# Two score maps of a head, placed in different rows of the TensorE array and issued by turns

## The chip, the core and the metric

The kernel runs on one core of a Trainium2 chip. The metric is the device time of one execution in microseconds (us). Times of the profile count from the start of the span of the profiled execution.

## What is computed

Two layers of an encoder trunk on 512 tokens of width 1024, all in float32. Each layer has a token mixer with four branches (differential attention, a pooling mixer, a short convolution, a gated DeltaNet) and then a channel mixer: a dense SwiGLU in the first layer, a mixture of 8 experts in the second. The change is in differential attention. Each of its 4 heads has two score maps with their own queries and keys, each of width 32, and the output takes one softmax minus a multiple of the other:

```
s1 = jnp.einsum('bqhd,bkhd->bhqk', qa, k1).astype(F32) * scale + bias
s2 = jnp.einsum('bqhd,bkhd->bhqk', qb, k2).astype(F32) * scale + bias
a = jax.nn.softmax(s1, axis=-1) - lam * jax.nn.softmax(s2, axis=-1)
return jnp.einsum('bhqk,bkhd->bqhd', a.astype(v.dtype), v)
```

A block is 128 queries against all 512 keys.

## The kernel before

Activations lie with channels on the 128 partitions and tokens along the free dimension. A float32 product is made of three products of parts: each operand is split into a high part (H) and the rest (L), and H·H, H·L and L·H are added up in one PSUM tile. In projections these are lines 326, 327 and 328 (`mm3`), each on a 128x128 weight and 512 moving columns; in the score maps they are three passes of line 1155.

The queries of map 1 of all heads are one tile of 128 partitions (`aqH0`, `aqL0`), 32 partitions for each head; those of map 2 another (`aqH1`, `aqL1`); keys likewise (`akH`, `akL`). A pass of head h contracts over the partitions 32h to 32h+31, so it takes 32 rows of the array (`tile_position=(32 * h, 0)`) and all 128 of its columns. Both maps of a head use the same 32 rows.

`attention` goes over 4 heads and 4 blocks of queries: 16 blocks in a layer, 32 in both, with 64 maps and 192 passes. In a block, for each map: three passes into a PSUM tile `pt` (a pool of four), then on VectorE (DVE) the bias is added and the row's extreme is found in one operation (line 1160, `asc`), then ScalarE (ACT) takes the exponential and its sum (line 1162). When both maps are there: reciprocals (1165, 1166), a scaling on ACT (1167), the weighted sum on DVE (1168, again `asc`), four transposes on TensorE (1171) and the copy of their result (1173). After four blocks of two heads follow the products with the values (1178), where the two heads of a pair take different 64 columns of the array, and a normalisation (1186, 1196).

So that TensorE has work while DVE and ACT go through this chain, `self.fill()` takes steps from a list of generators (`set_fill` in `mixer`): projections of the other branches, six matmuls of 128x512 a step, with their conversions of weights (292 on ACT and 293 on DVE, `wH` and `wL`) and their later work on DVE, ACT and GpSimd (POOL). A block calls `self.fill(FILL_A)`, with FILL_A = 1, after each map and after the transposes. Once attention is done `end_gens` and later stages take the steps that are left, so their sum is fixed. The code's order is not the order on the engines: the instructions are put in order for each engine when the kernel is built, and on each engine that order is then kept.

The order of the weights' columns in `w_in`, which decides the partition that each query and key lands on, is prepared by `lay` on the host.

Of the kernel before, what the change touches and what calls it, by code (L numbers as in the profile page):

```python
# [17 lines left out]
P = 128  # L18
# [47 lines left out]
FILL_A = 1  # L66
# [67 lines left out]
def col(a):  # L134

    a = np.asarray(a)
    return np.moveaxis(a.reshape(a.shape[:-1] + (-1, P)), -1, 0).reshape(P, -1)


def chunks(w, width):  # L140

    K, M = w.shape
    return np.ascontiguousarray(w.reshape(K // P, P, M // width, width).transpose(2, 1, 0, 3)).reshape(
        M // width, P, -1)
# [8 lines left out]
def lay(inp):  # L153

    f = {k: np.asarray(v) for k, v in inp.items()}
    vec = np.zeros((P, NV), np.float32)

    def put(name, a):
        vec[:, V_OFF[name]:V_OFF[name] + a.shape[1]] = a

    half = np.arange(P) // 64
    put("c", col(f["c"][0]))
    put("ada_b", col(f["ada_b"]))
    put("mix_pre", col(f["norm_mix_pre"]))
    put("mix_post", col(f["norm_mix_post"]))
    put("ffn_pre", col(f["norm_ffn_pre"]))
    put("ffn_post", col(f["norm_ffn_post"]))
    put("b_merge", col(f["b_merge"]))
    put("pool_scale", col(f["pool_scale"]))
    put("sconv_w", np.moveaxis(f["sconv_w"].reshape(NL, 3, 2, P), -1, 0).transpose(0, 1, 3, 2).reshape(P, -1))  # L170
    put("dconv_w", np.moveaxis(f["delta_conv_w"].reshape(NL, 5, 6, P), -1, 0).transpose(0, 1, 3, 2).reshape(P, -1))
    put("subln", np.tile(f["diff_subln"].T, (2, 1)))
    put("dnorm", np.tile(f["delta_norm"].T, (2, 1)))
    for name, key in (("a_log", "delta_a_log"), ("dt_bias", "delta_dt_bias")):
        a = f[key].reshape(NL, 2, 2, 2)
        a = np.repeat(a.transpose(3, 0, 1, 2)[:, :, :, None, :], 2, 3)
        put(name, a[half].reshape(P, -1))
    put("lam", np.broadcast_to(f["diff_lambda"].reshape(1, -1), (P, NL * 128)))
    put("router_b", np.broadcast_to(f["router_b"][0][None], (P, NE)))
    cst, mcst = shape_constants()  # L180
    o = {"vec": vec, "cst": cst, "mcst": mcst,
         "rcst": np.concatenate([np.tile(np.arange(T)[None], (P, 1)), np.arange(P)[:, None] < np.arange(P)[None]],
                                1).astype(np.float32),
         "dist": np.abs(np.arange(P)[:, None] + 384 - np.arange(896)[None]).astype(np.float32)}
    o["x"] = np.ascontiguousarray(f["x"][0].T.reshape(KT, P, T).transpose(1, 0, 2)).reshape(P, KT * T)

    o["ada_w"] = np.ascontiguousarray(f["ada_w"].reshape(NL, D, 6 * KT, P).transpose(0, 2, 3, 1)).reshape(-1, P, D)

    by_hpar = lambda w: w.reshape(2, 2, 64, -1).transpose(1, 0, 2, 3).reshape(256, -1)

    def w_in(l, n, s):
        w = f["w_in"][l][:, s:s + 256]
        return np.ascontiguousarray(by_hpar(w.T).T if n == "dz" else w)
    o["w_in"] = np.concatenate([chunks(w_in(l, n, s), 256) for l in range(NL) for n, s in WIN_ORDER])
    o["w_bg"] = np.stack([chunks(np.ascontiguousarray(f["w_in"][l][:, 2816:2832]), 16)[0] for l in range(NL)])
    o["w_gb"] = np.concatenate([chunks(np.concatenate([f["w_merge"][l, i], by_hpar(f["w_branch"][l, i]) if i == 3
                                                   else f["w_branch"][l, i]]), 256)
                                for l in range(NL) for i in range(4)])
    o["w_o"] = np.concatenate([chunks(f["w_o"][l], 256) for l in range(NL)])
    pw = np.zeros((NL, 2, P, P), np.float32)  # L200
    for l in range(NL):
        for t in range(2):
            for s in range(2):
                pw[l, t, 64 * s:64 * s + 64, 64 * s:64 * s + 64] = f["pool_w"][l, 2 * t + s]
    o["pool_w"] = np.ascontiguousarray(pw.transpose(2, 0, 1, 3)).reshape(P, -1)
    o["ffn_g"] = chunks(f["ffn_w_gate"][0], 256)
    o["ffn_u"] = chunks(f["ffn_w_up"][0], 256)
    d = f["ffn_w_down"][0].reshape(NF // 2, 2, P, 2, 512)
    o["ffn_d"] = np.ascontiguousarray(d.transpose(0, 2, 3, 1, 4)).reshape(NF // 2, P, 2048)
    o["router_w"] = chunks(f["router_w"][0], NE)[0]  # L210
    g = f["moe_w_gate"][0].reshape(NE, 2, 4, P, NF // 2, 256).transpose(0, 4, 1, 3, 2, 5)
    u = f["moe_w_up"][0].reshape(NE, 2, 4, P, NF // 2, 256).transpose(0, 4, 1, 3, 2, 5)
    gu = np.stack([g, u], 5)
    dn = f["moe_w_down"][0].reshape(NE, NF // 2, 1, 2, P, D).transpose(0, 1, 2, 4, 3, 5)
    o["moe_w"] = np.concatenate([gu.reshape(NE, NF // 2, 2, P, 2048), dn.reshape(NE, NF // 2, 1, P, 2048)],
                                2).reshape(NE * 33, P, 2048)
    return o
# [14 lines left out]
class Enc:  # L232
# [899 lines left out]
    def attention(self, l):  # L1132
        nc = self.nc
# [5 lines left out]
        for pr in range(2):  # L1139
            AT = []  # L1140
            for hh in range(2):
                h = 2 * pr + hh
                bias = ap.tile([P, 896], FT, name="abias", bufs=1)
                nc.scalar.activation(bias, dist, AF.Copy, scale=-SLOPES[h])
                at = ap.tile([P, 4, T], FT, name=f"AT{hh}", bufs=1)
                AT.append(at)
                hs = slice(32 * h, 32 * h + 32)
                for qb in range(4):
                    qs = slice(qb * P, qb * P + P)
                    ex, sm = [], self.small.tile([P, 2], FT, name="asum")  # L1150
                    for i in range(2):
                        p = self.pt()
                        q, k = self.qk["q", i], self.qk["k", i]
                        for n, (x, y) in enumerate(((0, 0), (0, 1), (1, 0))):
                            nc.tensor.matmul(p, q[x][hs, qs], k[y][hs, :], start=n == 0, stop=n == 2,
                                             tile_position=(32 * h, 0))
                        self.fill(FILL_A)
                        s = ap.tile([P, T], FT, name="asc", bufs=4)
                        mx = self.small.tile([P, 1], FT, name="amx")
                        nc.vector.tensor_tensor_reduce(s, p, bias[:, 384 - 128 * qb:896 - 128 * qb], -1.0, 3e38,  # L1160
                                                       op0=OP.add, op1=OP.min, accum_out=mx)
                        nc.scalar.activation(s, s, AF.Exp, scale=-1.0, bias=mx, accum_out=sm[:, i:i + 1])
                        ex.append(s)
                    r = self.small.tile([P, 2], FT, name="arc")
                    nc.vector.reciprocal(r, sm)
                    nc.vector.tensor_tensor(r[:, 1:2], r[:, 1:2], self.nlam, op=OP.mult)
                    nc.scalar.activation(ex[1], ex[1], AF.Copy, scale=r[:, 1:2])
                    nc.vector.scalar_tensor_tensor(ex[0], ex[0], r[:, 0:1], ex[1], op0=OP.mult, op1=OP.add)
                    p = self.pt()
                    for kb in range(4):  # L1170
                        nc.tensor.transpose(p[:, kb * P:kb * P + P], ex[0][:, kb * P:kb * P + P], self.ident)
                    self.fill(FILL_A)
                    nc.vector.tensor_copy(at[:, :, qs], p.rearrange("p (b q) -> p b q", b=4))
            p = self.pt()
            for kb in range(4):
                for hh in range(2):
                    h = 2 * pr + hh
                    nc.tensor.matmul(p[64 * hh:64 * hh + 64], self.vt[:, kb, h * 64:h * 64 + 64], AT[hh][:, kb],
                                     start=kb == 0, stop=kb == 3)
# [15 lines left out]
            for b in range(4):  # L1195
                nc.tensor.matmul(pR[:, b * P:b * P + P], rb[:, b].rearrange("p a b -> p (a b)"), self.ident,
                                 start=True, stop=True)
# [1210 lines left out]
```

## Time and profile before

| | |
|---|---|
| Median of three runs | 2623.91 us (2621.54 to 2633.97) |
| Profiled execution: time | 2639.6 us |
| Profiled execution: span | 2637.8 us |
| TensorE (PE) busy | 2503.0 us, 95% of the span |
| DVE, ACT busy | 1605.7 us, 1213.4 us |
| Mean granted TensorE clock | 0.971 of full speed |

The span runs from the first to the last instruction that the profiler recorded; the execution's own time lies 1.8 us above it. TensorE's matmuls are pipelined: one of 512 columns is shown with some 390 ns, though the next starts 230 ns after it. So what a matmul costs the engine is read from start to start, not from the time beside it. A row names the engine, the line of the kernel, the tile written and the tiles read; the passes of a map are the rows of line 1155, and `asc` is written by both 1160 and 1168.

### The profile page before, as it was taken

What the parts mean: (1) busy time and instruction counts of PE and PEld (TensorE: products, weight loads), DVE (VectorE), ACT (ScalarE), POOL (GpSimd) and SP (SyncE); (2) the same over time, 40 slices, a digit from 0 to 9 for tenths busy, and PEclk for the clock granted to TensorE, in tenths of its full rate; (3) what the DMA queues carried; (4) which work ended last, traced back from release to release, by engine and by line L of the source; (5) the groups of instructions that cost most, each with busy time, mean ns of one, the idle gap of its engine ahead of it and who ended that gap; (6) DMA issues with size and microseconds to landing.
All of it is one profiled execution on the core that took longest, in us unless ns stands there. A gap on an engine that the chain in (4) does not pass through costs nothing. (4 is left out here: it accounts for less than half of the span.)

```text
span 2637.8 us, 42408 instructions
## 1 busy us (share of the span) xinstructions
PE 2503.0 (95%) x16106; PEld 2031.3 (77%) x16106; DVE 1605.7 (61%) x2914; ACT 1213.4 (46%) x2153; POOL 306.0 (12%) x304
## 2 busy tenths in 40 slices
PE   7999989989999989999899979999999999999996
PEld 6677767889888788677678878887766767799885
DVE  7666843576555565674734656665565556876685
ACT  4454333433333354544333525554444446765574
POOL 0101321241000021103222110000000001000111
PEclk8999999999999999999899989999999999999998
DMA  7113222454566443121222329557879888975681
GB/s 264 48 65 118 70 71 71 133 192 155 184 200 213 149 149 107 49 66 51 62 79 71 114 92 350 196 206 293 323 294 348 319 315 341 389 270 216 236 319 64
DMA packets 124564, 478.32 MB, mean 181 GB/s; under 512 B 14224, under 2 KB 16912, under 8 KB 97600
## 3 DMA queue, kind: packets, MB, share of 16 engines
q1 hardware_dynamic: 119808, 460.19, 48.8%
q0 software_dynamic: 4544, 15.34, 1.7%
q8 instruction: 128, 2.10, 0.3%
q14 instruction: 84, 0.69, 0.1%
HBM read 462.17 MB, written 13.30 MB: 180 GB/s over the span
## 5 line engine op out<-in xcount | busy, mean ns | idle before, releaser
L326 PE MATMUL mm<-hH,wH 128*128 128x512 f32 (+1 forms) x1264 | 490.4, 390 | 9.0 <-ACT hH L1044 4.8
L328 PE MATMUL mm<-hH,wL 128*128 128x512 f32 (+1 forms) x1264 | 481.7, 381 | 4.4 <-DVE wL L293 4.3
L327 PE MATMUL mm<-hL,wH 128*128 128x512 f32 (+1 forms) x1264 | 481.4, 381 | 1.2 <-DVE hL L1277 1.2
L1842 DVE TENSOR_TENSOR mL<-mraw,mH 128x1024 fp32r<-128x1024 f32 x286 | 343.8, 1222 | 178.3 <-ACT mH L1841 127.0
L292 ACT ACTIVATE wH<-raw 128x512 fp32r<-128x512 f32 (+3 forms) x400 | 246.4, 624 | 433.6 <-PE mm L327 318.1
L293 DVE TENSOR_TENSOR wL<-raw,wH 128x512 fp32r<-128x512 f32 (+3 forms) x400 | 280.0, 716 | 214.1 <-ACT wH L292 210.3
L1841 ACT ACTIVATE mH<-mraw 128x1024 fp32r<-128x1024 f32 x286 | 297.6, 1054 | 153.8 <-PE gu L1865 48.4
L1864 PE MATMUL gu<-hH,mH 128*128 128x384 f32 (+1 forms) x1056 | 313.5, 365 | 2.6 <-DVE hL L1800 1.7
L326 PEld LDWEIGHTS mm<-hH,wH 128*128 128x128 f32 x1264 | 241.7, 191 | 65.7 <-issue 9.9
L328 PEld LDWEIGHTS mm<-hH,wL 128*128 128x128 f32 x1264 | 242.1, 192 | 57.1 <-DVE wL L293 7.2
L327 PEld LDWEIGHTS mm<-hL,wH 128*128 128x128 f32 x1264 | 243.0, 192 | 44.8 <-issue 3.5
L1865 PE MATMUL gu<-hH,mL 128*128 128x192 f32 (+1 forms) x1056 | 268.2, 254 | 0.0
L1864 PEld LDWEIGHTS gu<-hH,mH 128*128 128x128 f32 x1056 | 198.9, 188 | 15.6 <-issue 8.5
L1865 PEld LDWEIGHTS gu<-hH,mL 128*128 128x128 f32 x1056 | 202.2, 192 | 0.8
L1864 PE MATMUL gu<-hL,mH 128*128 128x384 f32 (+1 forms) x704 | 195.6, 355 | 0.0
L1842 DVE TENSOR_TENSOR mL<-f,mH 128x512 fp32r<-128x512 f32 x220 | 140.3, 685 | 73.3 <-ACT mH L1841 57.5
L1865 PE MATMUL gu<-hL,mL 128*128 128x192 f32 (+1 forms) x704 | 172.6, 245 | 0.0
L1841 ACT ACTIVATE mH<-f 128x512 fp32r<-128x512 f32 x220 | 126.4, 621 | 63.0 <-PE gu L1865 39.1
L1864 PEld LDWEIGHTS gu<-hL,mH 128*128 128x128 f32 x704 | 132.6, 188 | 9.1 <-issue 4.9
L1865 PEld LDWEIGHTS gu<-hL,mL 128*128 128x128 f32 x704 | 135.1, 192 | 1.6 <-issue 0.8
L335 DVE CUSTOM_DVE_ANT_0 adr<-adr,ada 128x1024 f32<-128x1024 f32 x56 | 68.6, 1224 | 106.4 <-DMA adr<-in_ada_w 106.4
L326 PE MATMUL mm<-mH,ma 128*128 128x512 f32 (+1 forms) x308 | 126.4, 410 | 0.4 <-ACT ma L1882 0.4
(643 smaller groups left out, 4456.5 us busy)
## 6 DMA issues: line engine op xcount, KB each, us to landing
mraw<-in_moe_w SPq DMA_DIRECT2D x209, 1024.0 KB, 9.6
f<-in_moe_w SPq DMA_DIRECT2D x220, 256.0 KB, 6.8
raw<-in_w_gb SPq DMA_DIRECT2D x64, 640.0 KB, 3.9
adr<-in_ada_w SPq DMA_DIRECT2D x56, 512.0 KB, 3.4
raw<-in_w_in SPq DMA_DIRECT2D x40, 512.0 KB, 3.7
raw<-in_ada_w SPq DMA_DIRECT2D x32, 512.0 KB, 4.3
raw<-in_ffn_d SPq DMA_DIRECT2D x58, 256.0 KB, 3.5
raw<-in_ffn_g SPq DMA_DIRECT2D x24, 512.0 KB, 4.6
```

The source lines that it names most:

```text
L292: self.nc.scalar.activation(h, part, AF.Copy)
L293: self.nc.vector.tensor_tensor(l, part, h, op=OP.subtract)
L326: t.matmul(out, W[0], X[0], start=start, stop=False)
L327: t.matmul(out, W[0], X[1], start=False, stop=False)
L328: self.last_mm = t.matmul(out, W[1], X[0], start=False, stop=stop).ins
L335: self.nc.vector.tensor_tensor_reduce(r, r, self.sc, 1.0, 0.0, op0=OP.mult, op1=OP.add, accum_out=t[:, m:m + 1])
L1841: self.mark(self.nc.scalar.activation(h[:, s], x, AF.Copy))
L1842: self.mark(self.nc.vector.tensor_tensor(l[:, s], x, h[:, s], op=OP.subtract))
L1864: t.matmul(pp[i][:, f, :2 * n], w[0], X[k][:, :, :n], start=k == 0, stop=False)
L1865: self.mark(t.matmul(pp[i][:, f, :n], w[1], X[k][:, 0, :n], start=False, stop=k == KT - 1))
```

## The change

Two edits. On the host the columns of the queries and keys of the second map are rolled by 32 within their 128, so that head h of the second map lies on the partitions of 32((h+1) mod 4), while the first map keeps 32h. In `attention` both PSUM tiles are taken first, the six passes of the two maps are issued by turns (pass 1 of map 1, pass 1 of map 2, pass 2 of map 1, ...), and the two single filling steps behind the maps become one call for two steps behind both. What follows for each map is as it was.

```
     def w_in(l, n, s):
         w = f["w_in"][l][:, s:s + 256]
+        if n in "qk":
+
+            w = np.concatenate([w[:, :P], np.roll(w[:, P:], 32, 1)], 1)
...
-                hs = slice(32 * h, 32 * h + 32)
+                row = [32 * h, 32 * ((h + 1) % 4)]
                 for qb in range(4):
                     qs = slice(qb * P, qb * P + P)
                     ex, sm = [], self.small.tile([P, 2], FT, name="asum")
-                    for i in range(2):
-                        p = self.pt()
-                        q, k = self.qk["q", i], self.qk["k", i]
-                        for n, (x, y) in enumerate(((0, 0), (0, 1), (1, 0))):
-                            nc.tensor.matmul(p, q[x][hs, qs], k[y][hs, :], start=n == 0, stop=n == 2,
-                                             tile_position=(32 * h, 0))
-                        self.fill(FILL_A)
+                    pp = [self.pt() for _ in range(2)]
+                    for n, (x, y) in enumerate(((0, 0), (0, 1), (1, 0))):
+                        for i in range(2):
+                            q, k = self.qk["q", i], self.qk["k", i]
+                            hs = slice(row[i], row[i] + 32)
+                            nc.tensor.matmul(pp[i], q[x][hs, qs], k[y][hs, :], start=n == 0, stop=n == 2,
+                                             tile_position=(row[i], 0))
+                    self.fill(2 * FILL_A)
+                    for i, p in enumerate(pp):
                         s = ap.tile([P, T], FT, name="asc", bufs=4)
```

The added lines move the numbers below them: 1155, 1160, 1168 and 1171 are 1159, 1165, 1173 and 1176 in the changed kernel, and 293, 326 to 328 and 935 are 296, 329 to 331 and 938.

On TensorE, at the second block of the first layer, the order before has two products of a filling projection between the maps (`akH_150` is of the first map, `akH_152` of the second):

```order
L1171 MATMUL pt<-cst,asc 128x128 x4
L1155 MATMUL pt<-akH_150,aqH_146 128x512
L1155 MATMUL pt<-akL_151,aqH_146 128x512
L1155 MATMUL pt<-akH_150,aqL_147 128x512
L327 MATMUL mm<-hL_84,wH 128x512
L328 MATMUL mm<-hH_83,wL 128x512
L1155 MATMUL pt<-akH_152,aqH_148 128x512
L1155 MATMUL pt<-akL_153,aqH_148 128x512
L1155 MATMUL pt<-akH_152,aqL_149 128x512
L326 MATMUL mm<-hH_85,wH 128x512
```

In the changed kernel the same place on TensorE reads:

```order
L1176 MATMUL pt<-cst,asc 128x128 x4
L1159 MATMUL pt<-akH_150,aqH_146 128x512
L1159 MATMUL pt<-akH_152,aqH_148 128x512
L1159 MATMUL pt<-akL_151,aqH_146 128x512
L1159 MATMUL pt<-akL_153,aqH_148 128x512
L1159 MATMUL pt<-akH_150,aqL_147 128x512
L1159 MATMUL pt<-akH_152,aqL_149 128x512
L329 MATMUL mm<-hH_83,wH 128x512
```

The two products have moved behind the maps. Counted over the whole order, 4 of the 16 blocks of each layer (the first four) have filling work between their two maps before, and the other 12 have their six passes side by side already; in the changed kernel all 16 have. The filling products between the last pass of a block and its transposes change too: in the first layer 16, 17, 20, 19, 16, 33, 21, 18, 28, 24, 18, 18, 26, 22, 23, 23 before, and 21, 20, 19, 24, 21, 26, 30, 20, 26, 27, 22, 20, 26, 22, 23, 23 now (the fourth with 38 small matmuls of another branch among them); in the second layer 18, 16, 25, 22, 23, 16, 19, 26 in the last eight before and 22, 18, 20, 25, 21, 20, 21, 26 now.

On DVE, in the third block of the first layer, the end of the block's chain stood behind two conversions before (`x_741` is of the pooling branch):

```order
L1166 TENSOR_TENSOR arc<-arc,nlam 128x1
L931 TENSOR_SCALAR x_741<-dy 64x512
L935 TENSOR_TENSOR x_741<-x_741,cst 128x8 x2
L293 TENSOR_TENSOR wL<-raw,wH 128x512
L1168 SCALAR_TENSOR_TENSOR asc<-asc,arc 128x512
```

In the changed kernel DVE has there:

```order
L1171 TENSOR_TENSOR arc<-arc,nlam 128x1
L934 TENSOR_SCALAR x_741<-dy 64x512
L1173 SCALAR_TENSOR_TENSOR asc<-asc,arc 128x512
L934 TENSOR_SCALAR x_741<-dy 64x512
L296 TENSOR_TENSOR wL<-raw,wH 128x512
L938 TENSOR_TENSOR x_741<-x_741,cst 128x8 x2
```

The weighted sum, for which the transposes wait, has come ahead of the weight conversion and of the two small products. The order is the same there in the second layer.

## Rows read from the trace of the kernel before

**Rows 1.** The page: the span, and TensorE's busy time, share and instructions.

```profile
span 2637.8 us, 42408 instructions
PE 2503.0 (95%) x16106; PEld 2031.3 (77%) x16106; DVE 1605.7 (61%) x2914; ACT 1213.4 (46%) x2153; POOL 306.0 (12%) x304
```

**Rows 2.** Both attention stretches: length; PE, PEld, DVE, ACT, POOL busy; clock; DMA.

```profile
65.16:211.60 146.44, 142.12 (x663) 101.91 (x662) 97.72 (x236) 73.50 (x147) 12.73 (x9) 0.97 0.18 60
1035.05:1182.50 147.45, 143.20 (x653) 102.33 (x652) 97.89 (x236) 73.98 (x147) 12.33 (x9) 0.94 0.17 55
```

**Rows 3.** Waits of TensorE, first attention stretch: us in total, times, longest.

```profile
PE pt L1171 <- DVE asc L1168: 2.9, 1, 2.9
```

**Rows 4.** Timeline of TensorE, second block, layer 1: start, duration, instruction.

```profile
73.74 0.50 PE L327 MATMUL mm<-hL,wH 128*128 128x512 f32 x1
74.08 0.40 PE L328 MATMUL mm<-hH,wL 128*128 128x512 f32 x1
74.40 0.49 PE L1155 MATMUL pt<-akH,aqH 32*128 32x512 f32 x1
74.74 0.39 PE L1155 MATMUL pt<-akL,aqH 32*128 32x512 f32 x1
74.97 0.39 PE L1155 MATMUL pt<-akH,aqL 32*128 32x512 f32 x1
75.29 0.50 PE L326 MATMUL mm<-hH,wH 128*128 128x512 f32 x1
```

**Rows 5.** Timeline of all engines, fifth block of layer 1, from first pass to transposes.

```profile
111.97 0.50 PE L1155 MATMUL pt<-akH,aqH 32*128 32x512 f32 x1
...
112.31 0.40 PE L1155 MATMUL pt<-akL,aqH 32*128 32x512 f32 x1
...
112.98 0.69 DVE L1160 CUSTOM_DVE_ANT_0 asc<-pt,abias 128x512 f32<-128x512 f32 x1 [0.21 <-PE pt L1155]
...
113.26 0.38 PE L1155 MATMUL pt<-akH,aqL 32*128 32x512 f32 x1
113.57 0.51 PE L327 MATMUL mm<-hL,wH 128*128 128x512 f32 x1
...
116.48 0.75 DVE L1168 SCALAR_TENSOR_TENSOR asc<-asc,arc 128x512 f32<-128x512 f32 x1 [0.85 <-ACT asc L1167]
...
117.36 0.38 PE L1171 MATMUL pt<-cst,asc 128*128 128x128 f32 x2
```

**Rows 6.** Line 1178: its durations (ns, min/median/max), then two groups of its timeline.

```profile
L1178 PE MATMUL pt<-AT,avt x64: 592/592/643, 141.0 to 1187.3; 128*64 128x512 f32 x64
...
1112.19 1.07 PE L1178 MATMUL pt<-AT,avt 128*64 128x512 f32 x2
...
1114.09 3.65 PE L1178 MATMUL pt<-AT,avt 128*64 128x512 f32 x14
```

**Rows 7.** Timeline of the third block of layer 1, the end of its chain.

```profile
86.34 0.72 ACT L1167 ACTIVATE asc<-asc,arc 128x512 f32<-128x512 f32 x1 [0.99 <-DVE arc L1166]
...
87.65 0.68 DVE L293 TENSOR_TENSOR wL<-raw,wH 128x512 fp32r<-128x512 f32 x1
...
88.25 1.55 DVE L1168 SCALAR_TENSOR_TENSOR asc<-asc,arc 128x512 f32<-128x512 f32 x1
...
89.85 0.66 PE L1171 MATMUL pt<-cst,asc 128*128 128x128 f32 x4 [2.90 <-DVE asc L1168]
```

**Rows 8.** Two stretches behind that block; columns as in Rows 2.

```profile
90.40:93.70 3.30, 3.30 (x9) 1.06 (x8) 0.63 (x4) 0.00 (x0) 3.04 (x3) 0.50 0.20 78
97.30:104.00 6.70, 6.70 (x28) 5.33 (x26) 2.50 (x11) 4.00 (x8) 0.00 (x0) 0.50 0.00 0
```

**Rows 9.** Timeline of the thirteenth block: DVE behind a projection, and the transposes.

```profile
185.06 0.69 DVE L966 TENSOR_TENSOR dpad<-cc,mm 128x512 f32<-128x512 f32 x1 [1.35 <-PE mm L328]
...
187.87 0.75 DVE L1168 SCALAR_TENSOR_TENSOR asc<-asc,arc 128x512 f32<-128x512 f32 x1
...
188.72 0.61 PE L1171 MATMUL pt<-cst,asc 128*128 128x128 f32 x4
```

## The prediction, made before the changed kernel ran

> **What bounds the kernel now.** Start with the page: TensorE is busy for 95% of the span [rows 1]. That share alone does not price a change to TensorE, so the next view is that of the stretches. The change acts only in two of them, the attention of each layer, 146.4 and 147.5 us long; TensorE is shown busy for 142.1 and 143.2 us there, DVE for 97.7 and 97.9 [rows 2]. Then the list of waits: in the first stretch TensorE waits 2.9 us for DVE's weighted sum, and once only [rows 3]. So TensorE sets the pace, and the filling work, whose sum is fixed, closes nearly every gap: what a block saves on TensorE lets everything behind it start earlier, unless the transposes then have to wait. How near they are to that, the timeline says. In the fifth block the weighted sum ends at 117.23 us and the transposes start at 117.36; in the thirteenth 188.62 and 188.72 [rows 5, 9]. The slack is a tenth of a microsecond: the chain through DVE and ACT is a second bound, just behind the first.
>
> **What a pass and a change of rows cost.** Read from start to start. A pass takes 0.23 us (74.74 to 74.97) [rows 4]. From a 128-row product to a pass it is 0.32, to the next pass 0.34; from the last pass to a product 0.32, and to the next product 0.34 [rows 4]. So each change between 32 and 128 rows costs 0.09 ahead of it and 0.11 behind it, 0.20 in all. In a block whose maps stand side by side the four steps from 112.31 to 113.26 take 0.95, or 0.24 each, with no step between the maps [rows 5].
>
> **The change, part by part.**
>
> *Fewer changes of rows.* In 8 of the 32 blocks filling work stood between the maps, which costs four changes; now there are two. 8 x 0.40 = 3.2 us, whatever else happens.
>
> *Two passes at once.* This term decides, and no row shows two products that take different rows and the same columns. Bounds: the lower is the passes as they are, one behind the other at 0.24, gain nothing. The upper is the nearest row with different tiles by turns, line 1178. Two of its instructions alone take 1.07 us, of 0.59 to 0.64 each, so the second starts 0.43 or more behind the first. Fourteen, the halves of the columns by turns, take 3.65 us; one behind another they would take 13 x 0.43 + 0.59 = 6.2 [rows 6]. So two tiles of the array do work at once. By that, six passes become three steps, and a block saves 3 x 0.24 = 0.71 us; if the second map's first weights lie open like the first's (0.11 [rows 4]), 0.60. I take 0.65, near the upper bound, since line 1178 is the only row where two tiles alternate, and nothing there is lost: 32 x 0.65 = 20.8 us. With the changes of rows, TensorE sheds 24.0 us (at most 25.9, at least 3.2).
>
> The Trainium skill ("TensorE: Matmul & The Clock Gate", part 3 on packing small matmuls) states for row tiles that products start about 4 ns apart and gives 3.07 times the throughput for four products of 32 rows and 512 columns; by that page a pair would cost one pass, 0.71 us less a block. The trace of before agrees for halves of columns and does not show it for rows.
>
> *The stall of the third block.* The weighted sum started at 88.25 us though ACT had finished its input at 87.06; a weight conversion from 87.65 and two small products stood ahead on DVE [rows 7]. Now they stand behind it. It can start up to 1.19 us earlier, in both layers, since the order is the same: 2.4 us (bounds: none, and twice the whole 2.9). What moves behind it, the weight conversion, is due next for a filling projection that comes only behind the next maps.
>
> *The clock.* Behind that stall the granted clock is 0.50 for 3.3 us and again for 6.7 us [rows 8], that is 1.2 of 2.4 GHz, and half of each stretch is lost, 5.0 us. TensorE had stood 2.9 us ahead of the first, and ahead of the second it ran small matmuls, which stay. I take no change; the bounds are 5 us either way.
>
> *What is given back.* The transposes come up to 0.65 us sooner than now and have 0.1 us of slack. Does the chain move too? In the fifth block it hangs on the first map: DVE started 1.01 us after the first pass, when the map's third pass was through [rows 5]. With overlap that pass is again the third step, so the chain stays where it is; but the order now has 21 products there in place of 16, 5 x 0.23 = 1.15 us of cover, and no wait appears. In the thirteenth block there are 26 products as before; but DVE itself sat 1.35 us waiting for a projection there [rows 9], and that projection comes earlier with TensorE, so the chain moves along. A block with neither help waits 0.65 - 0.10 = 0.55. Leaving out the third and fourth blocks, bounds over 28 blocks are 0 and 15.4 us. I take 0.25 each, a little under half, since both kinds of help are seen: 7.0 us.
>
> *At nothing:* the host's rolling of columns (same bytes, same transfers), and the two `pt` tiles taken at once (adjacent maps had two already, from a pool of four). The joined filling steps cost nothing while the sum of steps is fixed; if they left a gap, it would be in the give-back above.
>
> **The sum.** 24.0 + 2.4 - 7.0 = 19.4 us. Against the profiled execution, 2639.6 - 19.4 = 2620.2. That execution was 15.7 us above the median of the runs; off the median, 2623.9 - 19.4 = 2604.5, so **2605 us**, or 0.7% faster.
>
> **The rivals.**
>
> *The chain takes it back.* The passes overlap, but every block then waits for DVE: 24.0 - 15.4 = 8.6 us, 2615. For it: a slack of 0.1 us in both blocks read. Against: DVE is busy for only 67% of the stretches [rows 2], and most orders of the first layer's early blocks got longer cover. The Trainium skill ("TensorEngine Tiling (Array Packing)", section on the PSUM bottleneck) warns of just this: tiling speeds TensorE, not what empties PSUM. The rows above agree that the chain is next.
>
> *No overlap.* Both maps send results to all 128 columns; if that makes the second wait, only the switches and the stall's part remain, 3.2 + 2.4 = 5.6 us. Worse, by turns the first map is ready two steps later, 0.47 us, so the chains start later; the longer cover hides most of it. I leave 4 us: 2620. For it: no row shows shared columns. Against: the columns of line 1178 each have their own rows busy, all 128, so overlap as such is no rarity here.
>
> *Going from one row place to another costs like a change of rows.* Then each block has five more changes of 0.20 us: 32 x 5 x 0.20 = 32 us, less 5.6, so 2650, slower. It decides from 5.6 / 160 = 0.035 us a change. Against it: line 1178 changes its columns with every instruction and loses nothing [rows 6]. For it: a change of rows has its price today [rows 4].
>
> **Chances.** Forecast 0.60; chain takes it back 0.18; no overlap 0.15; slower 0.07. The forecast's own range: 25.9 + 2.4, 5 us of a clock that stays up and nothing given back make 2590.6; a give-back of 11 us makes 2608.5. The range for 8 in 10 reaches over the two weaker gains and leaves out the slower case and the extreme of the gains: **2594 to 2621**. About 0.5%, 13 us, is what a measurement of this kernel can tell from no change; only the forecast lies beyond it: faster 0.60, same 0.33 (the two weak cases), slower 0.07.
>
> **What would show it.** Overlap: in the timeline, the six passes of a block start in three pairs, some 0.24 us between pairs, and from first pass to first product it takes 0.9 us, not 1.6; without it the starts stay 0.24 apart, and with a price on changing places they lie 0.3 or more apart. The give-back: in TensorE's waits, line 1176 for `asc`, 7 us over both stretches if right, 15 if the rival is. The stall of the third block shrinks from 2.9 to under 2 us. Both attention stretches get some 10 us shorter; if they do and the time does not follow, a later stage took it. The forecast is wrong, above all, if a new wait of some 3 us in one block brings the clock down for several microseconds, or if the pairs do not start together.

## The result, and the profile after

The changed kernel takes 2619.09 us (median of 18 runs, 2614.5 to 2625.01), the kernel before 2633.16 (18 runs, 2621.54 to 2638.33). The ratio is 0.9947, 95% interval 0.9938 to 0.9957: 14.1 us or 0.53% faster. The forecast was 19.4 us off a median of three runs that lay 9.2 us under that of the eighteen. The profiled execution took 2621.0 us.

The page of the changed kernel, which answers to [rows 1], has the span and TensorE's busy time:

```profile
span 2619.2 us, 42410 instructions
PE 2478.2 (95%) x16106; PEld 2012.9 (77%) x16106; DVE 1599.8 (61%) x2914; ACT 1211.8 (46%) x2153; POOL 304.1 (12%) x304
```

TensorE issues as many instructions as before and is busy 24.8 us less. The timeline of TensorE in the second block of the first layer, the place of [rows 4], shows where; x2 means two instructions in one row:

```profile
69.59 0.49 PE L1159 MATMUL pt<-akH,aqH 32*128 32x512 f32 x2
69.93 0.39 PE L1159 MATMUL pt<-akL,aqH 32*128 32x512 f32 x2
70.16 0.40 PE L1159 MATMUL pt<-akH,aqL 32*128 32x512 f32 x2
70.49 0.50 PE L329 MATMUL mm<-hH,wH 128*128 128x512 f32 x1
70.82 0.39 PE L330 MATMUL mm<-hL,wH 128*128 128x512 f32 x1
```

The six passes start in three pairs, and from the first to the next product it takes 0.90 us; 1.60 before with maps side by side [rows 5]. In the trace the two starts of the first pair lie 4 ns apart.

The stretches of attention (length; PE, PEld, DVE, ACT, POOL busy; clock; DMA), which answer to [rows 2]:

```profile
62.50:200.80 138.30, 133.22 (x664) 95.13 (x662) 96.50 (x236) 72.81 (x147) 12.36 (x9) 0.95 0.19 63
1028.30:1163.10 134.80, 128.62 (x654) 91.54 (x652) 96.57 (x236) 72.78 (x147) 12.75 (x9) 0.96 0.19 60
```

They are 8.1 and 12.7 us shorter. TensorE's waits there (us in total, times, longest), the first layer's ahead of the second's, stand against the one of [rows 3]:

```profile
PE pt L587 <- DVE g L578: 2.4, 1, 2.4
PE pt L1201 <- DVE bt L1199: 1.4, 1, 1.4
PE pt L1176 <- DVE asc L1173: 1.0, 3, 0.6
...
PE pt L587 <- DVE g L578: 4.0, 1, 4.0
...
PE pt L1176 <- DVE asc L1173: 0.5, 1, 0.5
```

The stall of the third block is gone, and the transposes (line 1176) hardly wait. The first row of each layer is new: line 587 is the cumulated sums of the gates, small products of a filling branch, and it waits for `g` on DVE. (The row of line 1201 stands in both traces of the kernel before too, as line 1196 with 1.3 us.)

Where that wait comes from, the timeline of all engines shows, in the fourth block of the first layer, from its last pass on (in brackets the idle time before, and what ended it):

```profile
85.99 0.40 PE L1159 MATMUL pt<-akH,aqL 32*128 32x512 f32 x2
...
86.94 1.46 DVE L934 TENSOR_SCALAR x<-dy 64x512 f32<-64x512 f32 x1 [0.47 <-POOL dy L928]
88.09 1.47 POOL L928 TENSOR_TENSOR dy<-dy 128x513 f32<-128x513 f32 x1
...
89.59 0.42 DVE L934 TENSOR_SCALAR x<-dy 64x512 f32<-64x512 f32 x1 [1.17 <-POOL dy L928]
90.05 0.24 DVE L938 TENSOR_TENSOR x<-x,cst 128x8 f32<-128x8 f32 x2
90.38 1.28 POOL L939 TENSOR_TENSOR x<-x,dpad 128x512 f32<-128x512 f32 x1 [0.82 <-DVE x L938]
...
91.71 0.68 DVE L1165 CUSTOM_DVE_ANT_0 asc<-pt,abias 128x512 f32<-128x512 f32 x1 [1.41 <-issue]
91.72 0.06 DVE L608 MEMSET dpad<- 128x2 f32 x1
...
97.03 0.19 DVE L578 SCALAR_TENSOR_TENSOR g<-uu,nA 128x32 f32<-128x32 f32 x1
...
97.36 0.40 PE L587 MATMUL pt<-g,cst 64*64 64x16 f32 x6 [2.41 <-DVE g L578]
```

The maps are through at 86.4 us, but the bias step (line 1165) starts at 91.71. In the order built for DVE there stand ahead of it a step of the pooling branch (line 934), which waits for POOL's line 928, and then the clears of the padding of `dpad` (lines 608 and 609), which wait for POOL's line 939; so DVE idles while the finished maps lie there. Everything of the gates behind it is late too; `g` comes at 97.2, 10.9 us after the gates' first small products (86.32), and TensorE has run out of filling work 2.4 us earlier. Before, TensorE came to this block later, at 94.30 us. There `g` came 5.6 us after those products (95.62), and line 584, which is 587 of the changed kernel, found it ready:

```profile
100.98 0.19 DVE L575 SCALAR_TENSOR_TENSOR g<-uu,nA 128x32 f32<-128x32 f32 x1
...
105.50 0.43 PE L584 MATMUL pt<-g,cst 64*64 64x16 f32 x6
```

Three of the four windows of the stretches in which the granted clock is low (columns as in the stretches above), which answer to [rows 8]:

```profile
89.40:92.60 3.20, 3.20 (x9) 2.55 (x8) 1.56 (x8) 0.17 (x1) 1.44 (x2) 0.50 0.00 0
99.30:105.90 6.60, 6.60 (x19) 4.79 (x19) 3.03 (x9) 3.37 (x10) 0.00 (x0) 0.51 0.23 79
...
1062.00:1072.40 10.40, 9.85 (x37) 7.33 (x38) 5.08 (x16) 4.73 (x11) 0.00 (x0) 0.51 0.16 52
```

They are at 0.50 or 0.51, that is 1.2 of 2.4 GHz. The second lies 2 us behind the wait for `g`, and the third begins at the end of that wait in the second layer (line 587 starts at 1062.55). Ahead of the first TensorE ran 64 products of 4 columns from 86.32 to 88.28. The fourth, 3.4 us from 143.8 on, lies behind neither.

### The profile page after: what moved, and what is told of

It is laid out like the page before. It is cut to its first block, busy times and chain, and to the rows that moved or that the text cites. A ratio compares the mean times of both kernels' runs of the same rounds, so it can differ in the third digit from the quotient of the medians.

```text
span 2619.2 us, 42410 instructions
## 1 busy us (share of the span) xinstructions
PE 2478.2 (95%) x16106; PEld 2012.9 (77%) x16106; DVE 1599.8 (61%) x2914; ACT 1211.8 (46%) x2153; POOL 304.1 (12%) x304
```

## The experiments

Ratios are to the kernel before on the same chip, with 95% intervals. The two theories at the start: the gain is two passes running at once, and the issue by turns is what makes it (mine); or it comes from the new order of the filling work and of DVE (the rival). 

### Which part gives the time

**Other order, same rows.** The changed kernel without the rolling, so that both maps of a head have the same 32 rows. On every engine the order is that of the changed kernel.

```
-        if n in "qk":
-            w = np.concatenate([w[:, :P], np.roll(w[:, P:], 32, 1)], 1)
...
-                row = [32 * h, 32 * ((h + 1) % 4)]
+                row = [32 * h, 32 * h]
```

> The changed kernel with one thing taken back: both maps of a head lie in the same 32 rows again; the passes still go by turns, and every engine keeps the order of instructions of the changed kernel. Theory (two passes at once brings the gain): the six passes of a block take 1.6 us to the first product again in place of 0.9, so 32 x 0.69 = 22 us come back on TensorE, less some waits that vanish; 14 to 22 us slower than the changed kernel, ratio to the kernel before 0.999 to 1.004. Rival (the gain comes from the order: fewer changes of rows, the weighted sum ahead of the conversions): ratio stays at 0.995 to 0.997.

Measured: 2640.69 us, ratio 1.0009 (0.9995 to 1.0022). The timeline of TensorE in its second block:

```profile
76.64 0.72 PE L1159 MATMUL pt<-akH,aqH 32*128 32x512 f32 x2
77.21 0.62 PE L1159 MATMUL pt<-akL,aqH 32*128 32x512 f32 x2
77.68 0.62 PE L1159 MATMUL pt<-akH,aqL 32*128 32x512 f32 x2
```

Each pair now takes two steps, and the gain is gone: the order gives nothing by itself. The new wait is there: line 587 waits 0.2 and 1.8 us in the two layers, against 2.4 and 4.0. Part of that difference is the clock. From the gates' first small products to the last product ahead of line 587 TensorE has the same work, without a gap, in both layers of the changed kernel and, below, of this one (columns as in the stretches):

```profile
86.32:94.95 8.63, 8.63 (x87) 6.97 (x85) 4.92 (x22) 2.52 (x7) 4.52 (x4) 0.80 0.16 55
1051.48:1058.51 7.03, 7.03 (x87) 5.81 (x85) 3.62 (x13) 0.88 (x4) 4.55 (x4) 1.00 0.18 63
...
88.16:98.31 10.15, 10.15 (x86) 8.25 (x85) 5.38 (x24) 4.71 (x11) 3.81 (x3) 0.66 0.07 25
1066.58:1075.20 8.62, 8.62 (x86) 6.97 (x85) 4.88 (x21) 3.16 (x8) 3.84 (x3) 0.80 0.07 26
```

(x87 and x86 differ by the end of one pass that reaches into the window.) At full clock (1.00) it takes 7.03 us. What a lower clock adds comes off the wait, since `g` comes no later for it: 10.9 us after the first of those products in both layers of the changed kernel, 10.2 in both here. With that added back, line 587 would wait, by estimate, 4.0 us in both layers of the changed kernel and 3.3 in both layers here. So the wait belongs to the new order, and overlap makes it some 0.7 us a block longer, what it saves on the passes of one block.

**The same rows, one map behind the other.** As above, with the loops over `n` and `i` exchanged:

```
-                    for n, (x, y) in enumerate(((0, 0), (0, 1), (1, 0))):
-                        for i in range(2):
+                    for i in range(2):
+                        for n, (x, y) in enumerate(((0, 0), (0, 1), (1, 0))):
```

> Both maps in the same 32 rows, all three passes of the first map and then those of the second, the two filling steps behind both: the kernel before with only the filling moved. Theory (two passes at once brings the gain): only the changes of rows are saved, 8 x 0.40 = 3.2 us, and some of the stall: ratio to the kernel before 0.997 to 1.000. Rival (order brings it): 0.995 to 0.996.

Measured: 2634.52 us, 0.9993 (0.9979 to 1.0006). Issuing by turns on the same rows neither costs nor gives anything that shows. Line 587 waits 2.9 and 1.3 us.

**Both kernels again**, for a second trace of each.

> The changed kernel once more, for a second profile and on this chip. Theory (the 14 us of the medians are the attention stretches alone, and the 21 us that the two profiles show there are partly the luck of two executions): ratio 0.994 to 0.996, attention stretches within 4 us of 137.7 and 134.2. Rival (a later stage takes some 7 us back each time): stretches as before, and the part between the two attention stretches some 4 us longer than in the kernel before again.

> The kernel before once more, for a second profile. Ratio 0.999 to 1.001. If the first profile was a slow execution, its attention stretches of 145.9 and 147.0 us come out 2 to 5 us shorter here; if the attention gain of 21 us is steady, they stay, and what lies between them is shorter in the kernel before than in the changed one.

Measured: 2622.71 us, 0.9944 (0.9931 to 0.9957) for the changed one; 2635.05, 0.9995 (0.9983 to 1.0007) for the one before. Line 587 waits 4.1 and 2.4 us in the changed one, with the clock at 1.00 and 0.80 on the way there: the two layers have changed places. The stretches of the kernel before are these:

```profile
63.10:209.30 146.20, 141.95 (x664) 101.97 (x662) 98.17 (x236) 73.53 (x147) 12.74 (x9) 0.96 0.18 60
1039.40:1182.15 142.75, 138.49 (x654) 98.68 (x652) 97.81 (x236) 73.86 (x147) 12.33 (x9) 0.98 0.18 57
```

The second is 4.7 us shorter than in [rows 2], at a clock of 0.98 in place of 0.94. The stretches of the changed kernel add up to 273.1 us in both of its traces, so they are 20.8 us shorter than in the first trace of before and 15.9 shorter than in the second. Whether a later stage takes something back is not told by this: between the stretches lie 823 and 830 us before, 828 and 832 in the changed kernel.

**Other rows, one map behind the other.** The changed kernel with only the loops exchanged, as above.

> The second map in other rows as in the changed kernel, but all three passes of the first map come ahead of the three of the second: only the turns are taken back. Theory (the engine starts products in order, and one starts beside the one before it if that is in other rows): in a block only the second map's first pass can start beside the first map's third, one step of 0.24 us of six is saved in place of three, 32 x 0.24 = 7.7 us; ratio to the kernel before 0.996 to 0.998. Rival (the engine runs ahead by itself, turns are not needed): 0.994 to 0.995.

Measured: 2626.84 us, 0.9947 (0.9927 to 0.9967). The whole gain stays, against my theory, and the timeline of TensorE says why:

```profile
110.40 0.50 PE L1159 MATMUL pt<-akH,aqH 32*128 32x512 f32 x2
110.74 0.40 PE L1159 MATMUL pt<-akL,aqH 32*128 32x512 f32 x2
110.97 0.40 PE L1159 MATMUL pt<-akH,aqL 32*128 32x512 f32 x2
111.30 0.50 PE L331 MATMUL mm<-hH,wL 128*128 128x512 f32 x1
```

These are passes 1, 2 and 3, each of both maps, though in the order built for TensorE all three of the first map stand ahead of the second's. The second map's first pass starts at 110.411, 10 ns behind the first map's first and 0.33 us ahead of the first map's second (110.741). The Trainium skill ("TensorE: Matmul & The Clock Gate", Part 3, The mechanism) says that products start strictly in the program's order; this trace differs, and it decides. (The order built for DVE and ACT shifts a little with the loops: line 587 waits 3.5 and 3.6 us, the transposes 2.5 and 3.7.)

**The rows alone.** The kernel before with the rolling and the second map's row place; the order of every engine stays that of before.

```
-                hs = slice(32 * h, 32 * h + 32)
+                row = [32 * h, 32 * ((h + 1) % 4)]
...
-                                             tile_position=(32 * h, 0))
+                                             tile_position=(row[i], 0))
```

> The kernel before with the rows alone: the second map of a head lies in other rows, and nothing is moved; every engine keeps the order of the kernel before. Theory (TensorE starts a product ahead of its turn when its rows are free, so neither turns nor the joined filling are needed for the overlap): in the 24 blocks whose maps stand side by side the six passes start in three pairs, 24 x 0.70 = 17 us less on TensorE; but that order holds fewer products between maps and transposes, and the waits of TensorE for the weighted sum grow by 4 to 10 us: ratio to the kernel before 0.995 to 0.998. Rival (it needs the joined filling and the order that comes with it): 0.998 to 1.0.

Measured: 2626.74 us, 0.9950 (0.9934 to 0.9967), not told apart from the change itself. In the 24 blocks whose maps stood side by side the passes overlap. Steps added up, TensorE sheds 16.4 us, but the waits of the transposes grow. In the first layer (line 1174 is 1176 of the changed kernel):

```profile
PE pt L1174 <- DVE asc L1171: 4.3, 5, 2.9
```

The stall of the third block (2.9) stays, and 1.4 us come to it; so does the second layer with 4.3 us over 4. Its line of the cumulated sums doesn't wait in either layer. The new order of the changed kernel therefore does two things that nearly cancel: it joins the maps of eight blocks and removes that stall, and it brings the wait for `g`.

### Where the rest went

**Cumulated sums later.** If the wait for `g` is lost time, line 587 must come later. The branch is cut at that line, and its second half is due behind the keys' branch.

```
-FILL_ORD = "pbkzqsv"
+FILL_ORD = "pbkBzqsv"
...
+        self.dl = dict(beta=beta, g=g)
+        self.bg_sm = sm
+        yield
+
+    def g_bg2(self):
```

> The changed kernel with one other thing moved: the 12 small products of the gates' cumulated sum (line 587), for which TensorE waits 2.4 and 4.0 us in the changed kernel, are a filling step of their own, two projections later. Theory (a new wait for the gates took back 6.4 us and the clock behind it some 3): 5 to 10 us faster than the changed kernel, ratio to the kernel before 0.9905 to 0.9925. Rival (the waits only move to the transposes of the same block, whose sum hangs on the same DVE queue): 0.994 to 0.995, and the wait of line 1176 grows by what line 587 lost.

Measured: 2623.9 us, 0.9926 (0.9902 to 0.9951), which overlaps the interval of the changed kernel: not settled by the time. The waits, first layer (line 1183 is 1176):

```profile
PE pt L1183 <- DVE asc L1180: 2.8, 2, 2.2
```

Most of the 2.4 us has moved to the next thing that needs the late bias step, the transposes; so it is in the second layer, with 3.0 us.

**And the clears on GpSimd.** Besides, the branches' clears of `dpad` go from DVE to GpSimd.

```
-            nc.vector.memset(pad[:, 0:2], 0.0)
+            nc.gpsimd.memset(pad[:, 0:2], 0.0)
```

> As the one with the cumulated sum later, and the four clears of padding columns go from DVE to GpSimd, so that DVE's queue no longer stands behind the pooling branch's work on GpSimd in the fourth block, where the bias step came 5.7 us after the maps in the changed kernel. Theory (the fourth block's chain is held up by the clears, in order on DVE): the bias step there comes within 2 us of the maps, and another 2 to 6 us go; ratio to the kernel before 0.988 to 0.992. Rival (GpSimd, now with the clears as well, holds up what comes next): no better than 0.9925.

Measured: 2618.39 us, 0.9918 (0.9900 to 0.9936). The bias step comes earlier, but not within 2 us of the maps; DVE's timeline (line 941 is 934 of the changed kernel, 1172 is 1165):

```profile
86.58 1.47 DVE L941 TENSOR_SCALAR x<-dy 64x512 f32<-64x512 f32 x1 [0.47 <-POOL dy L935]
89.23 0.42 DVE L941 TENSOR_SCALAR x<-dy 64x512 f32<-64x512 f32 x1 [1.19 <-POOL dpad L616]
...
89.85 0.69 DVE L1172 CUSTOM_DVE_ANT_0 asc<-pt,abias 128x512 f32<-128x512 f32 x1
```

The last pass ends at 86.0; the bias step starts 3.8 us later (5.3 in the changed kernel), still behind the pooling branch's wait for POOL. With line 587 moved, the largest wait of the transposes is 0.8 us in the first layer and 2.4 in the second, where no half clock lies ahead of it (3.4 us do in the first). The ratio's interval ends at 0.9936, just below the 0.9938 where the changed kernel's first one begins; its second, from 0.9931, overlaps. A gain of 0.3% over the changed kernel is likely, not shown.

**Four maps at once.** If row places run side by side, four should. Both heads of a pair go together: second maps rolled by 64, the four tiles taken at once, twelve passes by turns; the second head's bias is written over `dist`.

```
-            w = np.concatenate([w[:, :P], np.roll(w[:, P:], 32, 1)], 1)
+            w = np.concatenate([w[:, :P], np.roll(w[:, P:], 64, 1)], 1)
...
-                row = [32 * h, 32 * ((h + 1) % 4)]
+                row.append([32 * h, 32 * ((h + 2) % 4)])
...
+                pp = [[self.pt() for _ in range(2)] for _ in range(2)]
```

> Twice the dose: the four maps of two heads lie in the four row places and their twelve passes go by turns, then four filling steps, then the two chains one behind the other. Theory (row places work at once, four like two): twelve passes take three steps, 0.9 us to the first product in place of 2 x 0.9, so 16 x 0.9 = 14 us more go from TensorE; the chain of two blocks is longer than the filling and gives 0 to 10 back: ratio to the kernel before 0.987 to 0.995. Rival (results of four row places to the same columns do not fit, or weights for four do not load in a step): twelve passes take six steps and the ratio is 0.994 to 1.0.

Measured: 2610.74 us, 0.9891 (0.9875 to 0.9907). TensorE's timeline:

```profile
105.95 0.54 PE L1160 MATMUL pt<-akH,aqH 32*128 32x512 f32 x4
106.29 0.43 PE L1160 MATMUL pt<-akL,aqH 32*128 32x512 f32 x4
106.52 0.43 PE L1160 MATMUL pt<-akH,aqL 32*128 32x512 f32 x4
106.89 0.50 PE L329 MATMUL mm<-hH,wH 128*128 128x512 f32 x1
```

Twelve passes take three steps, 0.94 us in all with the change of rows. A new wait again takes its part, the first row of TensorE's waits in the first layer:

```profile
PE pt L557 <- ACT dth L546: 2.9, 1, 2.9
```

Line 557 is the gates' first small products, which wait for ACT; 2.8 us in the second layer.

**Four maps, with the late sums and the clears on GpSimd.**

> Four maps at once as before, with the gates' cumulated sum as a filling step of its own two projections later and the clears of padding on GpSimd. Theory (what is left of the four maps' waits hangs on the gates' chain and on DVE standing behind the pooling branch): 2 to 8 us faster than four maps alone, ratio to the kernel before 0.986 to 0.988. Rival (the wait of 2.9 us for the gates' first small matmuls, which stay where they were, is the one that counts): 0.988 to 0.990.

Measured: 2612.05 us, 0.9900 (0.9882 to 0.9918), no different from four maps alone. The wait of line 557 stands unmoved at 2.9 us; what was mended was not what waited here.

**Four maps, the gates' first products a step of their own as well.** With the edits of the last kernel, and two places later in the filling order, so that ACT has time for `dth`:

```
-FILL_ORD = "pbkzqsv"
+FILL_ORD = "pbkcqBzsv"
...
+    def g_bg1(self, l):
```

> As four maps with the cumulated sum later, and the gates' first small matmuls, for which TensorE waited 2.9 and 2.8 us with four maps, also become a filling step of their own, one projection later. Theory (that wait and the clock behind it cost 5 to 9 us in both layers): ratio to the kernel before 0.984 to 0.987, and no wait of TensorE over 1.5 us in either attention stretch. Rival (the chain through DVE and ACT is the bound by now): 0.987 to 0.989, with the waits of the transposes grown instead.

Measured: 2605.47 us, 0.9885 (0.9865 to 0.9905; four runs), within the noise of four maps alone, and the lowest median of all. It lies where the rival had put it (0.987 to 0.989), though the interval reaches into the theory's range. The wait of line 557 is gone, and those of the transposes have grown from 1.9 and 1.2 us in the two layers to 2.7 and 2.5; the first layer's:

```profile
PE pt L1190 <- DVE asc L1187: 2.7, 3, 1.4
```

## Why the prediction came out as it did

Steps from start to start on TensorE, added up over both stretches, before (second trace) against after (first):

| Term | forecast, us | seen, us |
|---|---|---|
| passes and the changes of rows around them | -24.0 | 55.7 to 31.6: -24.1 |
| gaps ahead of the transposes, third block's stall among them | -2.4 + 7.0 | 13.9 to 12.1: -1.8 |
| wait of line 587 for `g` | 0 | 2.4 + 4.0: +6.4 |
| clock (half of the time at 0.50) | 0 | 17.1 to 23.9: +3.4 |
| steps around the transposes | 0 | +1.2 |
| sum | -19.4 | -14.9 |

The medians say -14.1, and the stretches of these two traces -15.9. Against the first trace of before the stretches give -20.8 and the span -18.6, near the forecast. That is luck: the other terms agree within 0.3 us in both traces of before, but the first was at half clock for 27.3 us in the stretches.

*Two passes at once, and fewer changes of rows:* right, within 0.1 us of 24.0. Line 1178, with its columns by turns [rows 6], was a fair guide to rows by turns. The busy time of the passes alone, in windows around the two stretches, says the same. Before:

```profile
60.00:215.00 155.00, 27.52 (x96) 0.97 0.18 61
1020.00:1190.00 170.00, 28.00 (x96) 0.95 0.18 58
```

And after, 22.8 us less for the same 192 passes:

```profile
60.00:215.00 155.00, 16.57 (x96) 0.96 0.21 68
1020.00:1190.00 170.00, 16.15 (x96) 0.97 0.17 54
```

*The stall of the third block:* right in kind and too small. The weighted sum came ahead of the conversion, and all of the 2.9 us a layer went, not 1.2.

*What is given back:* this is the step that failed in kind. I put 7.0 us on the transposes of 28 blocks and left out the third and fourth. The transposes give back some 4 us (5.8 of stall gone, gaps only 1.8 shorter), with waits of 1.0 and 0.5 us in the list. The loss is in the fourth block, which I had left out: 6.4 us of a filling branch's product that waits for DVE, which itself stands behind POOL. The joined filling steps were put at nothing "while the sum of steps is fixed", but it is not only how many: line 587 now stands where its input isn't ready. That the order brings most of it is shown by the same rows by turns, which wait there without overlap, and by the rows alone, which overlap in the old order and don't wait there. The number hides this error: with the stall I forecast 7.0 - 2.4 = 4.6 us given back, and 6.4 - 1.8 = 4.6 were seen. That is luck.

*The clock:* "no change" is the step that failed in the sum; most of the 5.3 us by which the forecast gain was too large lies here, as far as is known. Single traces can't tell: at half clock in the stretches were 27.3 and 17.1 us in the two traces of before and 23.9 in each of the changed kernel, so the row of the table is +3.4 us against the second trace and -1.7 against the first. The mean granted clock of whole executions tells more. For the kernel before it is 0.9752 (29 runs) and between 0.9747 and 0.9760 in three smaller sets, for the changed one 0.9734 (18 runs) and 0.9732 (5 runs); the standard errors of the 29 and the 18 are 0.0004. A clock lower by 0.0018 over 2620 us is 9.4 us more at half clock, by estimate 4.7 us of time; with that in place of 3.4 the sum is -13.6, and it lies just inside the prediction's bounds of 5 us. Where in the execution it falls the runs don't say. The lower clock goes with the new order and not with overlap: the rows alone stay at 0.9753 (6 runs, 0.9755 before), and the same rows by turns, with order and wait but without overlap, have 0.9722 (12 runs). That the wait for `g` is what brings it down is argued from where the low stretches lie, not shown: four maps at once wait 2.9 us for `dth` and have 0.9752 (6 runs). The prediction named a new wait of some 3 us with the clock behind it as what would make it wrong, but did not price it into the sum.

*The base:* the forecast of 2605 is 14.6 us under the time; 5.3 of that is the gain, and 9.2 the median of three runs. So the larger part of the miss is not the change at all.

*The rivals:* none took place. "The chain takes it back" priced 15.4 us on the transposes, which wait 1.5. "No overlap" falls with the pairs. A price for changing places would have shown in the steps from pair to pair; they are 0.34 and 0.23 us, as with one place [rows 4]. Its sign would have been seen also in the rows alone, which are faster.

What stays open: the 1.2 us around the transposes, what in the new order lowers the clock, and whether the late bias step could be brought to the maps by giving the pooling branch another place; that wasn't tried.

## What to carry to other kernels

When one engine sheds time, look not only at the chain that the change touches but at every consumer that now comes sooner, filling work too: price the wait of each against the in-order queue of its producer, and the clock behind the wait. Give small products that contract over 32 rows different row places, four if there are four; the order in which they are issued mattered little here, but the slack of what comes next did. And take the base from more than three runs when the forecast is of half a per cent.

## What the runs showed of the hardware

- TensorE started products of one row place ahead of products that were issued earlier for another: 110.411 us against 110.741 with the maps one behind the other.
- Two row places took three steps for six passes, and four took three for twelve (0.94 us to the next product), all writing all 128 columns. The starts of the four lie 3, 4 and 38 ns apart, and twelve passes take 0.94 us where three took 0.89 (74.40 to 75.29 [rows 4]). The Trainium skill ("TensorE: Matmul & The Clock Gate", Part 3, Measured speedup vs the span model) gives 3.07 times for four products of 32 rows and 512 columns; the trace agrees that four run at once.
- A lower clock ahead of a wait for another engine cost nothing: the same work of TensorE took 8.63 us at 0.80 and 7.03 at 1.00, and the wait behind it was 2.4 us and 4.0.
- Changing from one row place to another had no price that shows, though a change between 32 and 128 rows costs 0.20 us [rows 4].
